# Pinning the accumulating transfers of the summed weights behind the GpSimd work named ahead of them

## The chip, the cores and the metric

The kernel runs on one core of one Trainium2 chip. The time is the device time of one execution in microseconds (us). It is measured in several runs, and the median counts. The core has five engines that run side by side, each working through its own queue in order: TensorE (PE, matrix products), VectorE (DVE), ScalarE (ACT), GpSimd (POOL) and SyncE (SP, which here only starts transfers). Transfers between main memory (HBM) and the on-chip memory (SBUF) are done by DMA engines; a queue starts them and goes on.

## The reference

A decoder trunk of two layers over 512 positions with 1024 channels in float32. Layer 0 mixes positions by causal mean pooling, layer 1 by attention in a sliding window of 128. Each mixer is followed by a gated MLP with a causal convolution of width 3:

```python
def conv_glu_ffn(h, w_in, conv_w, conv_b, w_out):
    u = h @ w_in                                  # 1024 -> 2 * 2816
    c = causal depthwise conv of u, width 3, + conv_b
    a, g = c[..., :D_FF], c[..., D_FF:]
    return (a * jax.nn.silu(g)) @ w_out           # 2816 -> 1024
```

Every mixer and every MLP reads `rms_norm(h, g) = h / sqrt(mean(h*h) + 1e-6) * g` and is added to `h`; a last norm closes the trunk.

## The kernel before

The activations lie with the 1024 channels on the partitions, as eight tiles `h0` to `h7` of 128x512. TensorE works on pairs: each float32 operand is split into a rounded part `h` and the rest `l`, and `mm3` (L83 to L87) makes one product of three matmuls: L85 is h times h, L86 and L87 are the cross terms. The split of a weight tile of 128x1024 is done in `weights` (L94): a transfer on SyncE's queue brings the raw tile (L91, a ring of three buffers), ScalarE copies it to the rounded part (L99), and VectorE subtracts to get the rest (L102). The split tiles have rings of four buffers each. For the first four weight tiles of layer 0 the subtraction is done on GpSimd instead, each in four pieces of 256 columns (`early_weights`, L319).

The norm before the MLP isn't applied ahead of the products. The activations are only scaled by the gain and split (`split_scaled`, L242 on ScalarE and L243 on VectorE, tiles `f0x_h` and `f0x_l`), and the factor 1/sqrt is multiplied in after the products. It comes from `Norm`: `add` squares each `h` tile on ScalarE (L212 for the first, L206 for the others, with two buffers `sq`) and adds it to one tile `n_acc` on GpSimd (L215, seven adds); `stats` sums over the channels by eight small matmuls on TensorE (L221) and takes the inverse root on VectorE (L181 to L195, `rs_` tiles); `spread` makes a diagonal of it (L231) and spreads it over the partitions by matmuls (L232) and a copy (L235).

`mlp_in` (L366) forms the 44 output tiles of `w_in`. In layer 0 it takes the first four weight tiles in two groups of two, and then one tile at a time. After the second group the statistics are issued (L395), after the fifth tile the spread (L397); only then can the products of these five tiles leave their banks (L358: times the factor, then the convolution, L361 to L363).

The product with `w_out` is done in three stretches (`GROUPS`), and two of them in each layer use sums of weight blocks and seven products of half size in place of eight (`mlp_sums`, L459). Their weights come from `sum_weights` (L438), four times for each stretch, sixteen times in all. It fills a tile `u` by a transfer on SyncE's queue (L447), and a second transfer, started by GpSimd, adds other blocks onto it while it is brought in (L450, `accum_op=ALU.add`). It therefore needs that L447 has landed. Tiles `r` and `q` come by L448 and L449. GpSimd then adds `u` and `r` into a tile `v` (L453, L454), and all four are split.

The order in each queue isn't the program's. A scheduler inside the compiler goes through the program with a model of how long instructions and transfers take, and gives each engine what is ready first in that model. On the chip each engine then works strictly in the order it was given, and waits where the model was wrong. `pin = tc.keep_in_program_order` (L116) binds one instruction behind the instruction that the program names last before it on the same engine. It orders the two in the queue and adds no wait. The instructions of the pooling mixer on ScalarE and VectorE are pinned in an order written out by hand (L341); the adds of the norm (L352) aren't, and neither are the transfers of L450.

Of the kernel before, what the change touches and what calls it, by code (L numbers as in the profile page):

```python
# [23 lines left out]
ALU = mybir.AluOpType  # L24
# [34 lines left out]
def trunk(ctx: ExitStack, tc: tile.TileContext, x_tok, x_t, vecs, w_pool, w_kq, w_v, w_o, w_in, w_out, w_sums, out_a, out_b):  # L59
    nc = tc.nc  # L60
    V, A, G, T = nc.vector, nc.scalar, nc.gpsimd, nc.tensor
# [32 lines left out]
    def weights(src, n, name, eng=None, raw=None, step=1024, pin=lambda ins: ins):  # L94

        raw = raw or fetch(src, n, name)
        h = wp.tile([P, 1024], F32R, tag="wh", name=f"{name}_h")
        l = wp.tile([P, 1024], F32R, tag="wl", name=f"{name}_l")
        pin(A.activation(h[:, :n], raw[:, :n], AF.Copy))  # L99
        for a in range(0, n, step):  # L100
            o = slice(a, min(a + step, n))
            (eng or V).tensor_tensor(l[:, o], raw[:, o], h[:, o].bitcast(F32), ALU.subtract)  # L102
        return h, l
# [7 lines left out]
    def out_weights(layer, m):  # L111
        n = 2 * GROUPS[layer][-1][0]
        w = weights(w_out[layer][m], n * P, f"wo{layer}_{m}")
        return [part(w, k) for k in range(n)]

    pin = tc.keep_in_program_order  # L116
# [38 lines left out]
    for g, w in enumerate(WINDOWS):  # L155
        b = band[:, g, :]
# [281 lines left out]
    def sum_weights(fp, layer, g, p, n):  # L438

        src = w_sums[layer][g][p]  # L440
        w = n * P
        name = f"ws{layer}_{g}_{p}"
        v = fp.tile([P, 1024], F32, tag="uv", name=f"{name}_u_raw", bufs=4)
        u, v = v, fp.tile([P, 1024], F32, tag="uv", name=f"{name}_v_raw", bufs=4)
        r = wp.tile([P, 1024], F32, tag="raw", name=f"{name}_r_raw", bufs=3)
        q = wp.tile([P, 1024], F32, tag="raw", name=f"{name}_q_raw", bufs=3)
        nc.sync.dma_start(u[:, : 2 * w].rearrange("p (a b) -> p a b", a=2), src[:, 0:4:2, :])  # L447
        nc.sync.dma_start(r[:, : 2 * w].rearrange("p (a b) -> p a b", a=2), src[:, 0:2, :])  # L448
        nc.sync.dma_start(q[:, :w], src[:, 3, :])  # L449
        G.dma_start(u[:, : 2 * w].rearrange("p (a b) -> p a b", a=2), src[:, 2:4, :], accum_op=ALU.add)  # L450
        R = weights(None, 2 * w, f"{name}_r", raw=r)
        Q = weights(None, w, f"{name}_q", raw=q)
        G.tensor_tensor(v[:, :w], u[:, w : 2 * w], r[:, :w], ALU.add)  # L453
        G.tensor_tensor(v[:, w : 2 * w], v[:, :w], r[:, w : 2 * w], ALU.add)  # L454
        W = weights(None, 2 * w, f"{name}_v", raw=v)
        U = weights(None, 2 * w, f"{name}_u", raw=u)
        return R, Q, W, U

    def mlp_sums(fp, layer, g, n, z):  # L459

        for p in range(NC // 2):
            R, Q, W, U = sum_weights(fp, layer, g, p, n)
            ba, be, bf = (bank("ps") for _ in range(3))
            lo, hi = slice(0, HS), slice(HS, S)
            sn = fp.tile([P, S], F32, tag="sn", name=f"sn{layer}_{g}_{p}")

            def product(out, w, b, t, start=True, stop=True):
                for i in range(n):
                    x = tuple(y[:, t, :] for y in z[i])
                    mm3(out, part(w, b * n + i), x, start and i == 0, stop and i == n - 1, skip_group_check=True)  # L470

            product(ba[:, lo], R, 0, 0)
            A.activation(sn[:, lo], ba[:, lo], AF.Copy)
            product(bf[:, lo], R, 1, 1)
            product(be[:, lo], Q, 0, 6)
            product(ba[:, lo], W, 0, 5, start=False)
            A.activation(sn[:, hi], ba[:, lo], AF.Copy)
            product(bf[:, hi], W, 1, 2)
            product(be[:, hi], U, 1, 3)
            product(ba[:, lo], U, 0, 4, start=False)  # L480
            h1, h2 = h[2 * p], h[2 * p + 1]
            V.tensor_tensor(h1, h1, sn, ALU.add)
            V.tensor_tensor(h1, bf, h1, ALU.add)
            V.tensor_tensor(h1[:, hi], h1[:, hi], be[:, hi], ALU.subtract)
            V.tensor_tensor(h2, be, h2, ALU.add)
            h22 = h2.rearrange("p (a b) -> p a b", a=2)
            V.tensor_tensor(h22, h22, ba[:, None, lo].to_broadcast([P, 2, HS]), ALU.subtract)
# [40 lines left out]
    with tc.tile_pool(name="ap", bufs=2) as ap:  # L528
# [53 lines left out]
        for c in range(2):  # L582
            u = ap.tile([P, S], F32, name=f"ku{c}", bufs=1)
# [170 lines left out]
        for i in range(NU + 4):  # L754
            base = AHEAD + i * RATE
            have = max(i - 4, 0)
            if i < NU:
                n, b = units[i]
# [21 lines left out]
    with tc.tile_pool(name="fp1", bufs=2) as fp:  # L780
# [31 lines left out]
        w = {m: out_weights(1, m) for m in range(NB, NC)}  # L812
# [116 lines left out]
```

## Time and profile before

| | |
|---|---|
| median of 3 runs | 920.04 us (919.86 to 920.27) |
| profiled execution | 919.19 us |
| its span | 917.4 us |
| mean granted clock of TensorE | 0.995 |
| TensorE busy | 904.5 us, 99% |
| VectorE busy | 681.7 us, 74% |
| ScalarE busy | 459.6 us, 50% |
| GpSimd busy | 192.7 us, 21% |
| transfers of L450 | 16, of which 12 of 512 KB; median 5.4 us from issue to landing |

The profile records one execution. All its times are in us from the start of the span, unless marked ns. A row of the timeline reads: start, length, engine, line of the kernel, operation, output<-inputs, form, and how many instructions were merged ("x8"); in brackets the idle time of the engine before it and what ended that. A row of the waits reads: who waited for whom, us in total, times, longest. In a row of the chain of waits the two numbers are start and length. A row of windows gives the window, its length, the busy time (and instructions) of PE, PEld (TensorE's weight loads), DVE, ACT and POOL, then the clock granted to TensorE as a share of full speed, and the share and rate of the DMA engines. The releaser in brackets is inferred: where several things were waited for, it is the last one by the profile.

### The profile page before, as it was taken

The numbers are of one execution on the slowest core, as the hardware profiler recorded it, in microseconds if no ns is written. First come the engines' busy times: TensorE is split into PE (matmuls) and PEld (weight loads), VectorE is DVE, ScalarE is ACT, GpSimd is POOL, SyncE is SP. The second block draws the span as 40 slices with busy tenths as digits, with TensorE's granted clock in tenths as the row PEclk, the third lists the DMA queues.
The fourth block names the chain that finished last, engine by engine and source line by source line (L and its number), as shares of the span: only waits on it lengthen the run. The fifth ranks groups of instructions, "written<-read, shape, count | busy, mean of one in ns | idle before, by whom it ended". The sixth has DMA issues, their size and how long they took to land.

```text
span 917.4 us, 13114 instructions
## 1 busy us (share of the span) xinstructions
PE 904.5 (99%) x4956; PEld 787.4 (86%) x4956; DVE 681.7 (74%) x1085; ACT 459.6 (50%) x715; POOL 192.7 (21%) x280
## 2 busy tenths in 40 slices
PE   9989999999999999999999999999999999999996
PEld 8878889988899888888889888888998889888896
DVE  7469998688997667555887472999977888877633
ACT  7646554344454344535888351654543445444532
POOL 3620113000321000425765041003210112000023
PEclk9989999999999999999999999999999999999999
DMA  8432436522444422322110043334464325523202
GB/s 328 124 114 69 134 100 170 172 93 92 115 127 125 131 78 80 127 93 92 47 47 24 12 151 85 100 115 138 126 165 134 96 72 117 175 93 98 93 18 92
DMA packets 33071, 100.03 MB, mean 109 GB/s; under 512 B 3440, under 2 KB 6000, under 8 KB 33008
## 3 DMA queue, kind: packets, MB, share of 16 engines
q1 hardware_dynamic: 30704, 91.33, 30.1%
q0 software_dynamic: 2304, 7.87, 5.2%
q8 instruction: 39, 0.64, 0.3%
q14 instruction: 24, 0.20, 0.1%
HBM read 97.09 MB, written 2.10 MB: 108 GB/s over the span
## 4 chain that ended last, share of the span: by engine, by line
PE 93%; ACT 3%; POOL 2%; DVE 1%; issue 1%; ACTq 0%; DVEq 0%
PE bank L85 29%; PE bank L87 29%; PE bank L86 29%; PE bank L700 1%; PE bank L728 1%; POOL n_acc L215 1%; PE bank L287 1%; PE bank L254 1%; POOL wi_l L102 1%; ACT h L331 0%; ACT sc L716 0%; ACT f0x_h L242 0%; ACT px_h L242 0%; ACT wi_h L99 0%; PE bank L221 0%
## 5 line engine op out<-in xcount | busy, mean ns | idle before, releaser
L99 ACT ACTIVATE wi_h<-wi_raw 128x1024 fp32r<-128x1024 f32 x88 | 93.0, 1060 | 133.6 <-PE bank L86 124.2
L102 DVE TENSOR_TENSOR wi_l<-wi_raw,wi_h 128x1024 fp32r<-128x1024 f32 x84 | 104.2, 1247 | 46.4 <-ACT wi_h L99 45.4
L87 PE MATMUL bank<-f0x_h,wi_l 128*128 128x512 f32 x352 | 137.8, 391 | 0.0
L86 PE MATMUL bank<-f0x_l,wi_h 128*128 128x512 f32 x352 | 137.7, 391 | 0.0
L85 PE MATMUL bank<-f0x_h,wi_h 128*128 128x512 f32 x352 | 137.4, 392 | 0.0
L85 PE MATMUL bank<-f1x_h,wi_h 128*128 128x512 f32 x352 | 137.2, 390 | 0.0
L86 PE MATMUL bank<-f1x_l,wi_h 128*128 128x512 f32 x352 | 137.0, 389 | 0.0
L87 PE MATMUL bank<-f1x_h,wi_l 128*128 128x512 f32 x352 | 137.0, 389 | 0.0
L358 DVE TENSOR_TENSOR c_u<-bank,n_rb 128x512 f32<-128x512 f32 x88 | 59.9, 686 | 45.0 <-PE bank L87 44.9
L453 POOL TENSOR_TENSOR ws_v_raw<-ws_u_raw,ws_r_raw 128x512 f32<-128x512 f32 (+1 forms) x16 | 22.9, 1432 | 324.2 <-DMA ws_r_raw<-w_sums 192.7
L215 POOL TENSOR_TENSOR n_acc<-n_acc,n_sq 128x512 f32<-128x512 f32 (+1 forms) x28 | 39.4, 1407 | 245.5 <-ACT n_sq L206 242.7
L87 PEld LDWEIGHTS bank<-f0x_h,wi_l 128*128 128x128 f32 x352 | 66.5, 189 | 14.3 <-POOL wi_l L102 0.4
L86 PEld LDWEIGHTS bank<-f0x_l,wi_h 128*128 128x128 f32 x352 | 66.7, 189 | 13.7
L85 PEld LDWEIGHTS bank<-f0x_h,wi_h 128*128 128x128 f32 x352 | 66.7, 189 | 13.7
L87 PEld LDWEIGHTS bank<-f1x_h,wi_l 128*128 128x128 f32 x352 | 66.1, 188 | 13.9
L86 PEld LDWEIGHTS bank<-f1x_l,wi_h 128*128 128x128 f32 x352 | 66.1, 188 | 13.6
L85 PEld LDWEIGHTS bank<-f1x_h,wi_h 128*128 128x128 f32 x352 | 66.1, 188 | 13.5
L361 ACT ACTIVATE c_t<-c_u,vec 128x512 f32<-128x512 f32 x88 | 70.1, 807 | 13.6 <-DVE c_u L358 12.7
L363 DVE SCALAR_TENSOR_TENSOR c_t<-c_u,vec,c_t 128x510 f32<-128x510 f32 x88 | 68.2, 779 | 2.3
L362 DVE SCALAR_TENSOR_TENSOR c_t<-c_u,vec,c_t 128x511 f32<-128x511 f32 x88 | 69.1, 789 | 0.5 <-ACT c_t L361 0.4
L428 ACT ACTIVATE zh<-y 128x256 fp32r<-128x256 f32 (+2 forms) x44 | 37.3, 847 | 60.6 <-DVE y L410 54.3
L401 ACT ACTIVATE c_t<-c_t 128x512 f32<-128x512 f32 x44 | 27.7, 629 | 58.8 <-DVE c_t L363 58.7
(210 smaller groups left out, 2185.2 us busy)
## 6 DMA issues: line engine op xcount, KB each, us to landing
wi_raw<-w_in SPq DMA_DIRECT2D x88, 512.0 KB, 3.5
ws_u_raw<-w_sums SPq DMA_DIRECT2D x12, 512.0 KB, 3.7
ws_u_raw<-w_sums POOLq DMA_DIRECT2D x12, 512.0 KB, 5.4
ws_r_raw<-w_sums SPq DMA_DIRECT2D x12, 512.0 KB, 3.5
kq_raw<-w_kq SPq DMA_DIRECT2D x10, 512.0 KB, 3.3
wo_raw<-w_o SPq DMA_DIRECT2D x8, 512.0 KB, 3.3
wo_raw<-w_out SPq DMA_DIRECT2D x8, 512.0 KB, 3.3
ws_q_raw<-w_sums SPq DMA_DIRECT2D x12, 256.0 KB, 2.7
```

The lines of the kernel that those rows point to most:

```text
L85: T.matmul(ps, lhsT=wh, rhs=xh, start=start, stop=False, **kw)
L86: T.matmul(ps, lhsT=wh, rhs=xl, start=False, stop=False, **kw)
L87: T.matmul(ps, lhsT=wl, rhs=xh, start=False, stop=stop, **kw)
L99: pin(A.activation(h[:, :n], raw[:, :n], AF.Copy))
L102: (eng or V).tensor_tensor(l[:, o], raw[:, o], h[:, o].bitcast(F32), ALU.subtract)
L215: eng.tensor_tensor(self.acc[:, lo:hi], self.acc[:, lo:hi], sq[:, lo:hi], ALU.add)
L358: V.tensor_tensor(u, ps, rb, ALU.mult)
L361: A.activation(t, u, AF.Identity, bias=col(V_CB + layer * 2 * NF + m), scale=cw[2])
L362: V.scalar_tensor_tensor(t[:, 1:], u[:, : S - 1], cw[1], t[:, 1:], ALU.mult, ALU.add)
L363: V.scalar_tensor_tensor(t[:, 2:], u[:, : S - 2], cw[0], t[:, 2:], ALU.mult, ALU.add)
L401: A.activation(conv[1], conv[1], AF.Silu)
L428: A.activation(h, src, AF.Copy)
```

## The change

One call in `sum_weights` is wrapped in `pin`:

```diff
         nc.sync.dma_start(u[:, : 2 * w].rearrange("p (a b) -> p a b", a=2), src[:, 0:4:2, :])
         nc.sync.dma_start(r[:, : 2 * w].rearrange("p (a b) -> p a b", a=2), src[:, 0:2, :])
         nc.sync.dma_start(q[:, :w], src[:, 3, :])
-        G.dma_start(u[:, : 2 * w].rearrange("p (a b) -> p a b", a=2), src[:, 2:4, :], accum_op=ALU.add)
+        pin(G.dma_start(u[:, : 2 * w].rearrange("p (a b) -> p a b", a=2), src[:, 2:4, :], accum_op=ALU.add))
```

Each of the sixteen accumulating transfers is bound behind the GpSimd instruction that the program names last before it. For the first in each layer that is the last add of the norm before the MLP (L215), for the others the second add of the sums before (L454). Nothing else in the program differs; the scheduler goes through the program again with these sixteen bonds.

## The prediction

> **What bounds the kernel now.** I read the page first, then the waits of TensorE, then the chain of waits around the longest of them, and last the timelines of single engines there.
>
> ```profile
> span 917.4 us, 13114 instructions
> ...
> PE 904.5 (99%) x4956; PEld 787.4 (86%) x4956; DVE 681.7 (74%) x1085; ACT 459.6 (50%) x715; POOL 192.7 (21%) x280
> ...
> PE 93%; ACT 3%; POOL 2%; DVE 1%; issue 1%; ACTq 0%; DVEq 0%
> ```
>
> TensorE is the bound: busy 99% of the span, and 93% of the chain. Something that moves on GpSimd can change the time only where TensorE stands still or runs slowly. The waits of TensorE, all that the view lists:
>
> ```profile
> PE bank L221 <- POOL n_acc L215: 3.2, 1, 3.2
> PE bank L254 <- DVE warm L252: 2.2, 1, 2.2
> PE bank L837 <- ACT n_sq L206: 0.5, 1, 0.5
> ```
>
> L254 is the start and L837 the tail. In between TensorE waits once, 3.2 us, and for GpSimd: L221 is the statistics of the first feed-forward norm, which need the sum of squares that GpSimd builds at L215. The granted clock in the windows around that wait:
>
> ```profile
> 48.00:49.00 1.00, 0.34 (x2) 0.00 (x0) 0.38 (x2) 1.00 (x2) 1.00 (x1) 1.00 0.00 0
> ...
> 50.00:51.00 1.00, 0.00 (x0) 0.00 (x0) 0.34 (x1) 0.00 (x0) 1.00 (x1) 0.84 0.67 270
> ...
> 57.00:58.00 1.00, 1.00 (x5) 0.82 (x4) 0.76 (x6) 0.00 (x0) 0.00 (x0) 0.75 1.02 311
> ```
>
> The number after the five engines is the clock: it falls within 50 to 51 and is back within 57 to 58. So the stall costs its own length and slow matmuls behind it. The chain there, and the same two steps in layer 1, where TensorE didn't wait:
>
> ```profile
> 47.12 2.15 POOL n_acc L215
> ...
> 49.34 2.13 POOL n_acc L215
> ...
> 51.51 1.87 PE bank L221 x8
> ...
> 60.94 0.89 PE bank L232 x8
> ```
>
> ```profile
> 571.19 0.79 PE bank L221 x8
> ...
> 577.58 0.89 PE bank L232 x8
> ```
>
> L221 to L232 is the statistics and 24 matmuls. It takes 9.43 us in layer 0 (60.94 - 51.51) and 6.39 in layer 1 (577.58 - 571.19). The lowered clock thus costs 3.04 us.
>
> **What moves.** GpSimd's timeline:
>
> ```profile
> 33.69 1.04 POOL L450 DMA_DIRECT2D ws_u_raw<-w_sums  x1 [5.93 <-DVE f0x_l L243]
> 34.48 5.83 POOL L102 TENSOR_TENSOR wi_l<-wi_raw,wi_h 128x256 fp32r<-128x256 f32 x8
> 40.05 11.41 POOL L215 TENSOR_TENSOR n_acc<-n_acc,n_sq 128x512 f32<-128x512 f32 x7
> 108.43 1.78 POOL L453 TENSOR_TENSOR ws_v_raw<-ws_u_raw,ws_r_raw 128x512 f32<-128x512 f32 x1 [56.97 <-DMA ws_r_raw<-w_sums]
> ...
> 111.85 0.89 POOL L450 DMA_DIRECT2D ws_u_raw<-w_sums  x1
> ...
> 551.85 1.50 POOL L215 TENSOR_TENSOR n_acc<-n_acc,n_sq 128x512 f32<-128x512 f32 x1 [3.94 <-ACT n_sq L206]
> 553.54 0.90 POOL L450 DMA_DIRECT2D ws_u_raw<-w_sums  x1 [0.20 <-issue]
> ```
>
> There are 16 transfers of L450. The pin sets each behind the GpSimd instruction that the program names last before it: L454 of the sums before, or the last L215 of the norm. The second (111.85), the first of layer 1 (553.54) and the others stand there already. Only the very first moves: from before the eight L102 pieces and seven L215 adds to behind them. Nothing needs it before L453 at 108.43, so its 1.04 us, its transfer and any wait of its own lie in 57 us of idle GpSimd: cost nothing. Without that cover it would cost its row, 1 us.
>
> What it held up is the point:
>
> ```profile
> 26.40 1.35 POOL L102 TENSOR_TENSOR wi_l<-wi_raw,wi_h 128x256 fp32r<-128x256 f32 x1
> 26.41 0.74 DVE L243 SCALAR_TENSOR_TENSOR f0x_l<-h,vec,f0x_h 128x512 fp32r<-128x512 f32 x1
> ...
> 28.21 0.65 SPq L447 DMA_DIRECT2D ws_u_raw<-w_sums  x1
> ...
> 28.45 1.07 ACT L99 ACTIVATE wi_h<-wi_raw 128x1024 fp32r<-128x1024 f32 x1
> 29.05 0.74 DVE L243 SCALAR_TENSOR_TENSOR f0x_l<-h,vec,f0x_h 128x512 fp32r<-128x512 f32 x1
> ...
> 30.01 1.07 ACT L99 ACTIVATE wi_h<-wi_raw 128x1024 fp32r<-128x1024 f32 x1
> 30.16 0.75 DVE L243 SCALAR_TENSOR_TENSOR f0x_l<-h,vec,f0x_h 128x512 fp32r<-128x512 f32 x1 [0.36 <-ACT f0x_h L242]
> ...
> 31.73 2.08 DVE L243 SCALAR_TENSOR_TENSOR f0x_l<-h,vec,f0x_h 128x512 fp32r<-128x512 f32 x3 [0.81 <-ACT f0x_h L242]
> ```
>
> ```profile
> DMA to landing us min/median/max: 4.7/5.2/5.6
> ```
>
> The transfer adds onto a tile that SyncE's L447 fills, issued at 28.21. The view of that tile shows two landings between 24 and 60 us; L447's took the 4.7, so it ends at 32.9, a little before L450 starts at 33.69. The profile blames DVE's f0x_l, which ended at about the same time; I take the landing. The eight pieces queued behind it have their inputs from 29.52 (28.45 + 1.07) and 31.08. Had they gone then, they would begin 4.96 us earlier than 34.48.
>
> Not all of that is kept. A piece alone takes 0.70 us (40.05 - 34.48, over 8), but the one at 26.40 took 1.35, ending 0.60 behind the L243 that started beside it (26.41 + 0.74). Four L243 start at 30.16 and later, and one ends at 29.79. Costs to GpSimd: 0.27 for that tail, and per L243 between 0 and 0.75. I take 0.6 each, the excess of the 1.35 row (0.65) rounded down because gaps lie between them: 2.4. Net gain of GpSimd 4.96 - 0.27 - 2.4 = 2.3 us; bounds 1.7 and 4.7.
>
> [...]
>
> The seven adds then follow as before, just earlier: their squares on ScalarE wait for GpSimd, and the two DVE splits that collide with the last two adds (2.15 and 2.13 us against 1.30 for an earlier one in the chain) hang on those squares too, so the pattern moves along.
>
> ```profile
> 45.75 1.30 POOL n_acc L215
> ```
>
> The chain of adds ends at 51.47 - 2.3 = 49.2 instead of 51.47 (49.34 + 2.13). TensorE arrives when its second group of weights is done:
>
> ```profile
> 33.22 0.39 PE L86 MATMUL bank<-f0x_l,wi_h 128*128 128x512 f32 x1
> ...
> 47.95 0.39 PE L87 MATMUL bank<-f0x_h,wi_l 128*128 128x512 f32 x1
> ```
>
> That is 48.34. New idle time: 0.85 us, between 0 and 1.5. The DVE rows that the earlier pieces may push back are read by TensorE only later: the f0x_l begun at 31.73 is needed at 33.22, 0.75 us after its end (31.73 + 0.74), and the next two later still, so a delay of 0.6 is covered; where it isn't, it falls inside this same idle time.
>
> **The clock.** If TensorE stands for 0.85 us instead of 3.17, I expect no fall: the fall in 50 to 51 came over 2 us after TensorE stopped at 48.34. [...] No run here shows a gap near 1 us.
>
> **The step after.** With the clock kept, L232 comes 6.39 us after the statistics. What is late next is the DVE work between them:
>
> ```profile
> 53.42 0.16 DVE L181 TENSOR_SCALAR rs_v<-bank 128x4 f32<-128x4 f32 x1 [3.08 <-PE bank L221]
> 53.53 1.23 DVE L102 TENSOR_TENSOR wi_l<-wi_raw,wi_h 128x1024 fp32r<-128x1024 f32 x1
> ...
> 54.74 1.22 DVE L102 TENSOR_TENSOR wi_l<-wi_raw,wi_h 128x1024 fp32r<-128x1024 f32 x1
> ...
> 57.91 0.88 DVE L231 TENSOR_SCALAR n_d<-ident,n_r 128x128 f32<-128x128 f32 x4
> 61.84 1.23 DVE L102 TENSOR_TENSOR wi_l<-wi_raw,wi_h 128x1024 fp32r<-128x1024 f32 x1 [3.05 <-ACT wi_h L99]
> ```
>
> From L181 to the first of L231's four pieces' end is 4.7 us (57.91 + 0.22 - 53.42), against 5.6 of matmuls (6.39 - 0.79): covered by 0.9. Behind L232 the same work follows relative to TensorE, which never waits again before the tail, so the gain is kept to the end.
>
> **Sum.** 3.17 - 0.85 = 2.3 of idle time and 3.04 of clock: 5.35 us, bounds 4.7 (idle 1.5) and 6.2 (idle 0). The profiled execution is 919.19 us (span 917.4 and 1.8 around it) and would come to 913.8; it lies 0.85 under the median of 920.04. From the median: 914.7, own range 913.8 to 915.4.
>
> **Rivals.**
>
> *The clock still falls.* A gap near 1 us, followed by eight tiny matmuls, may be enough. Then only idle time is saved: 2.3 us, 917.7. For it: the fall came at most 2.7 us after TensorE stopped (48.34 to 51), so less than 3 us of rest are enough. Against: layer 1 runs the same eight without a fall. Chance 0.14.
>
> *The transfer wasn't what held GpSimd.* The profile names f0x_l for the 5.93 us. If the pieces are shut out by DVE until the last L243 ends at 33.81, they begin only 0.67 us earlier; the gap stays 2.5 us, the clock falls, 919.4. Against: the piece at 26.40 passed in between L243s. The case that the pin changes no order at all ends here too, at 920.0. Chance 0.12.
>
> *Slower: the order on DVE turns over.* Each engine's order comes from a compile-time model, and the pin gives it other times. The DVE split of the ninth weight (61.84) stands behind L231. It needs TensorE's fifth group to end. If the model sets it ahead of the norm's steps, TensorE waits at L232 for a split that itself starts 0.9 us (61.84 - 60.94) after TensorE got there: L232 at about 49.2 + 6.39 = 55.6 would become 55.6 + 0.9 + 1.23 + 2.1 of norm steps (57.91 - 53.42 less the two splits between) + 0.2 = 60.0. That is 0.9 before today's 60.94, but TensorE has stood 4.4 us, and slow matmuls of 3.0 follow: 2.1 slower, 922.1. It decides if the split leaves its place behind L231. Against: today the split stands 3 us behind. Chance 0.09, with other turns of order that cost as much.
>
> **How the numbers follow.** Forecast 0.65. Within 0.2% (918.2 to 921.9, about what a measurement of this kernel can tell from no change) lie the second rival and the worst of the first. Faster 0.78, same 0.13, slower 0.09. The range reaches from 913.4, a little under idle 0 for the spread of runs, to 918.6, which takes in the first rival with the gap at its bound of 1.5.
>
> **What would show it.** Right: L450's first start behind the seventh L215, at 48 to 50; the first late L102 near 29.6, pieces of 1.0 to 1.35 beside L243; TensorE's wait at L221 under 1.5 us; the clock at 1.00 from 47 to 58; L221 to L232 near 6.4. Wrong: a start of those pieces after 33, a wait at L221 over 2 us, or a new wait at L232.

## The result and the profile after

The changed kernel takes 913.3 us (median of 4 runs, 913.19 to 914.04), the kernel before 920.15 us beside it (4 runs, 919.86 to 920.91). The ratio is 0.9926, with an interval of 0.9909 to 0.9943. The forecast was 914.7 us with a range from 913.4: the direction and the place were right, and the time fell 0.1 us below the range. The queues of the two programs differ in one place only: on GpSimd, the first L450 stands behind the seven adds.

The profiled execution after took 913.19 us. Its page, with the same lines as before:

```profile
span 911.4 us, 13112 instructions
...
PE 901.2 (99%) x4956; PEld 784.7 (86%) x4956; DVE 684.0 (75%) x1085; ACT 459.8 (50%) x715; POOL 192.8 (21%) x280
...
PE 92%; POOL 2%; DMA 2%; ACT 1%; issue 1%; DVE 1%; SPq 0%; ACTq 0%; POOLq 0%; DVEq 0%
```

The span is 6.0 us shorter, and TensorE's busy time fell by 3.3 us for the same 4956 matmuls: some of them ran faster. The waits of TensorE:

```profile
PE bank L254 <- DVE warm L252: 2.2, 1, 2.2
PE bank L837 <- ACT n_sq L206: 0.5, 1, 0.5
PE bank L287 <- DVE sband L285: 0.3, 1, 0.3
PE bank L221 <- POOL n_acc L215: 0.2, 1, 0.2
```

The wait at L221 is down from 3.2 to 0.2 us. GpSimd's timeline shows why:

```profile
29.58 7.48 POOL L102 TENSOR_TENSOR wi_l<-wi_raw,wi_h 128x256 fp32r<-128x256 f32 x8 [1.84 <-ACT wi_h L99]
37.03 11.24 POOL L215 TENSOR_TENSOR n_acc<-n_acc,n_sq 128x512 f32<-128x512 f32 x7
48.20 1.05 POOL L450 DMA_DIRECT2D ws_u_raw<-w_sums  x1
```

The eight pieces start at 29.58 instead of 34.48, as soon as ScalarE has the rounded part. They take 7.45 us to the first add instead of 5.57, with VectorE at its L243 meanwhile:

```profile
30.15 0.78 DVE L243 SCALAR_TENSOR_TENSOR f0x_l<-h,vec,f0x_h 128x512 fp32r<-128x512 f32 x1 [0.37 <-ACT f0x_h L242]
31.71 3.36 DVE L243 SCALAR_TENSOR_TENSOR f0x_l<-h,vec,f0x_h 128x512 fp32r<-128x512 f32 x3 [0.79 <-ACT f0x_h L242]
```

The last three L243 take 3.36 us instead of 2.08. Both engines lose: GpSimd 1.88 us, VectorE 1.28. The chain and the clock there:

```profile
46.12 2.16 POOL n_acc L215
...
48.32 1.05 PE bank L221 x8
...
54.96 0.89 PE bank L232 x8
```

```profile
50.00:51.00 1.00, 1.00 (x6) 0.81 (x5) 1.00 (x3) 0.00 (x0) 0.00 (x0) 1.00 0.98 143
...
57.00:58.00 1.00, 1.00 (x6) 0.81 (x6) 1.00 (x3) 0.28 (x1) 0.00 (x0) 1.00 0.00 0
```

The statistics begin 3.19 us earlier (51.51 - 48.32), L221 to L232 takes 6.64 us instead of 9.43, and the clock stays at 1.00. Together 5.98 us by L232, and it is kept to the end: the last ScalarE step of the chain starts at 912.75 before and 906.77 after, 5.98 apart.

```profile
906.77 0.69 ACT ob L853
```

### The profile page after: what moved, and what is told of

Its sections match the earlier page's. It is cut to its first block, busy times and chain, and to the rows that moved or that the text cites. A ratio compares the mean times of both kernels' runs of the same rounds, so it can differ in the third digit from the quotient of the medians.

```text
span 911.4 us, 13112 instructions
## 1 busy us (share of the span) xinstructions
PE 901.2 (99%) x4956; PEld 784.7 (86%) x4956; DVE 684.0 (75%) x1085; ACT 459.8 (50%) x715; POOL 192.8 (21%) x280
## 4 chain that ended last, share of the span: by engine, by line
PE 92%; POOL 2%; DMA 2%; ACT 1%; issue 1%; DVE 1%; SPq 0%; ACTq 0%; POOLq 0%; DVEq 0%
PE bank L85 30%; PE bank L86 29%; PE bank L87 29%; PE bank L700 1%; PE bank L728 1%; POOL wi_l L102 1%; DMA h<-x_t 1%; POOL n_acc L215 1%; DMA wi_raw<-w_in 1%; ACT sc L716 0%; PE bank L232 0%; PE bank L221 0%; ACT q L611 0%; ACT wo_h L99 0%; SPq L131 0%
## 5 line engine op out<-in xcount | busy, mean ns | idle before, releaser
L102 DVE TENSOR_TENSOR wi_l<-wi_raw,wi_h 128x1024 fp32r<-128x1024 f32 x84 | 104.3, 1247 | 40.1 <-ACT wi_h L99 39.8
L215 POOL TENSOR_TENSOR n_acc<-n_acc,n_sq 128x512 f32<-128x512 f32 (+1 forms) x28 | 39.5, 1410 | 245.1 <-ACT n_sq L206 242.2
L362 DVE SCALAR_TENSOR_TENSOR c_t<-c_u,vec,c_t 128x511 f32<-128x511 f32 x88 | 71.2, 814 | 0.5 <-ACT c_t L361 0.4
```

Of the source, the lines that this page charges most:

```text
L215: eng.tensor_tensor(self.acc[:, lo:hi], self.acc[:, lo:hi], sq[:, lo:hi], ALU.add)
L362: V.scalar_tensor_tensor(t[:, 1:], u[:, : S - 1], cw[1], t[:, 1:], ALU.mult, ALU.add)
```

## The experiments

**What GpSimd waited for.** My theory was that L450, waiting for the landing of L447, held the pieces. The rival was that VectorE's f0x_l, which the profile named, or the issue itself did. The first experiment keeps a transfer at the old place, but one that waits for nothing: a plain transfer into `v`. It leaves out the first accumulation; the other transfers are pinned.

```diff
+        if (layer, g, p) == (0, 0, 0):
+            with tc.issue_after(last_piece[0]):   # last piece of the second weight tile
+                G.dma_start(v[:, : 2 * w]..., src[:, 2:4, :])
+        else:
+            pin(G.dma_start(u[:, : 2 * w]..., src[:, 2:4, :], accum_op=ALU.add))
```

> The first transfer of L450 stays at its old place, between the pieces of the second and the third weight tile, but is a plain transfer into the tile v that waits for nothing; the first accumulation is left out, and the other transfers are pinned as in the change. Theory (the wait for the landing of L447 was the cost): GpSimd issues it at about 27.8, in the idle time ahead of the third tile, the pieces start at 29.6 as in the changed kernel, TensorE waits at L221 for 0.2 to 0.5 us, 913 to 914 us. Rival (a transfer at this place is held up by VectorE's L243, or its issue itself is what holds GpSimd): it starts near 33 or takes several us, the pieces start after it, 919 to 921 us.

Measured: 913.53 us (4 runs), a ratio to before of 0.9936 (0.9921 to 0.9951). GpSimd's timeline (the added lines move L450 to L461):

```profile
27.81 0.76 POOL L461 DMA_DIRECT2D ws_v_raw<-w_sums  x1
29.71 7.49 POOL L102 TENSOR_TENSOR wi_l<-wi_raw,wi_h 128x256 fp32r<-128x256 f32 x8 [1.14 <-ACT wi_h L99]
```

The transfer goes at once, in idle time, and the pieces follow with their inputs. An L243 of VectorE ran beside it from 27.84 on. The transfer stands at the same place of GpSimd's queue as in the kernel before, and its wait is gone. So neither the place nor the issue cost anything here; the wait did.

The second experiment moves the landing: one more transfer on SyncE's queue ahead of L447.

```diff
+        if (layer, g, p) == (0, 0, 0):
+            nc.sync.dma_start(v[:, : 2 * w]..., src[:, 0:4:2, :])
         nc.sync.dma_start(u[:, : 2 * w]..., src[:, 0:4:2, :])
...
+        ins = G.dma_start(u[:, : 2 * w]..., src[:, 2:4, :], accum_op=ALU.add)
+        if (layer, g, p) != (0, 0, 0):
+            pin(ins)
```

(In these two kernels the second L447 is pinned on SyncE's queue as well, to keep it from moving up.)

> The first transfer of L450 accumulates as before and isn't pinned (the others are), but SyncE starts one more transfer of 512 KB, into v, right ahead of L447, so that L447 lands some 1.5 to 2 us later. The scheduler puts L450 behind the third tile's four pieces, ahead of the fourth's. Theory (L450 waits for the landing): it starts at 34.5 to 35.5 instead of 33.69, the fourth tile's pieces follow it and end near 38.5 to 39.5, TensorE waits at L221 for 1.4 to 2.5 us, 914.5 to 918.5 us by whether the clock falls. Rival (L450 waits for VectorE's f0x_l): it starts at 33.7 as before, the wait at L221 is about 0.5 us, 913.5 us.

Measured: 918.46 us (10 runs, 916.37 to 919.71), ratio 0.9987 (0.9977 to 0.9997). GpSimd's timeline, where L450 is L454, and SyncE's transfer into `u` in the part on DMA issues (its last number is us to landing):

```profile
30.02 3.80 POOL L102 TENSOR_TENSOR wi_l<-wi_raw,wi_h 128x256 fp32r<-128x256 f32 x4 [1.84 <-ACT wi_h L99]
36.67 1.04 POOL L454 DMA_DIRECT2D ws_u_raw<-w_sums  x1 [2.85 <-PE bank L85]
37.46 3.09 POOL L102 TENSOR_TENSOR wi_l<-wi_raw,wi_h 128x256 fp32r<-128x256 f32 x4
```

```profile
29.34 0.59 SPq L449 DMA_DIRECT2D ws_u_raw<-w_sums  x1
```

```profile
ws_u_raw<-w_sums SPq DMA_DIRECT2D x1, 512.0 KB, 6.7
```

The start moved by 3 us, from 33.69 to 36.67, as the landing did (29.34 + 6.7 = 36.04, against 32.9); both moved further than I expected, and TensorE waits 3.2 us instead of the 1.4 to 2.5 forecast. It starts 0.6 us behind the landing, and 0.8 before. VectorE's last L243 had ended at 35.03, 1.6 us earlier. The name in brackets changed from f0x_l to a matmul, neither of which has to do with it. The theory holds. With four pieces ahead of the transfer instead of none, TensorE waits as long as before; but the transfer also started 3 us later, so what this order alone would give is not shown.

**What a shorter wait does to the clock.** The next kernels put known amounts of work on GpSimd into the changed kernel. First, the transfer behind the pieces and ahead of the adds (all sixteen are bound behind the last piece, in place of the pin; the queues differ from those of the changed kernel in the place of the first alone):

```diff
+        with tc.issue_after(last_piece[0]):   # last piece of the fourth weight tile
             G.dma_start(u[:, : 2 * w]..., src[:, 2:4, :], accum_op=ALU.add)
```

> The first transfer of L450 stands behind the eight pieces of L102 and ahead of the seven adds, with its wait long over; all else as in the changed kernel. Theory: only its issue of 1.05 us is paid, the adds end at 49.3 instead of 48.28, TensorE waits at L221 for 1.25 us. If the clock stands a wait of that length: 914.3 us, and L221 to L232 takes 6.4 to 6.7 us. Rival (the clock falls already then): L221 to L232 takes 9.4 us, 917.2 us.

Measured: 916.41 us (4 runs), ratio 0.9965 (0.9952 to 0.9979). The wait, the chain (L226 and L237 are L221 and L232) and the windows:

```profile
PE bank L226 <- POOL n_acc L220: 1.2, 1, 1.2
```

```profile
50.08 1.05 PE bank L226 x8
...
58.32 0.89 PE bank L237 x8
```

```profile
52.00:53.00 1.00, 1.00 (x4) 0.81 (x3) 1.00 (x3) 0.00 (x0) 0.00 (x0) 0.58 0.08 33
53.00:54.00 1.00, 1.00 (x4) 0.72 (x4) 0.98 (x4) 0.00 (x0) 0.00 (x0) 0.50 0.43 94
...
55.00:56.00 1.00, 1.00 (x5) 0.81 (x4) 0.82 (x5) 0.00 (x0) 0.00 (x0) 0.71 1.10 197
```

The wait is as expected, 1.2 us, but the clock falls after it: L226 to L237 takes 8.24 us, between my two numbers. The lowered stretch is 0.84 us in the window from 52 ((1 - 0.58) / 0.5), 2 us, and 0.58 us in that from 55: 3.4 us. By the same sum over the rows of before (0.32 us in the window from 50, half clock from 51 to 57, 0.5 in that from 57) it lasted 6.8 us there, twice as long. In issue_before_adds it began 2 us after TensorE had resumed.

Then memsets ahead of the last add, two and four of them:

```diff
         for c in range(NC):
+            for _ in range(2 if c == NC - 1 else 0):   # and 4
+                pin(G.memset(dly, 0.0))
             norm.add(c)                                # adds of n0 pinned
```

> The changed kernel with two memsets of 128x512 on GpSimd ahead of the last add (about 0.9 us), the adds pinned in their order. [...] Rival (a wait near 1 us is enough for the clock): L221 to L232 9.4 us, 917.2 us.

Measured: 913.57 us (4 runs), ratio 0.9938 (0.9921 to 0.9955), the wait at L221 0.3 us. The wait near 1 us that this was to test didn't come about, since the memsets cost nothing:

```profile
46.15 1.10 POOL L356 MEMSET dly<- 128x512 f32 x2
47.22 1.29 POOL L215 TENSOR_TENSOR n_acc<-n_acc,n_sq 128x512 f32<-128x512 f32 x1
```

The last add took 2.16 us in the changed kernel (46.12 to 48.28), beside VectorE's split (L102, 45.50 to 47.11). Here VectorE is busy from 46 to 47.29, the memsets run beside that split, and the add behind them takes 1.29. As a test of the clock this run says nothing beyond a wait of 0.3 us; it does show what a memset and an add cost beside VectorE.

> The same with four memsets (about 1.9 us): TensorE waits at L221 for about 2.1 us. [...] Rival (the clock falls at about 2 us): L221 to L232 9.4 us, 918.1 us; then the two together place the point between them.

Measured: 915.42 us (4 runs, 914.26 to 916.68), ratio 0.9958 (0.9943 to 0.9974). TensorE waits 1.4 us instead of the 2.1 expected, and the clock doesn't fall: L223 to L234 (L221 and L232 here) takes 6.64 us. That is a longer wait than in issue_before_adds, and no fall. So I profiled both kernels once more.

> The kernel with four memsets, profiled once more. In its first profile TensorE waited 1.4 us at L221 and the clock stayed; its times lie from 914.26 to 916.68 us. Theory: with a wait of this length it is a matter of where the windows of the clock lie, execution by execution, so the same kernel falls in some executions (L221 to L232 8.2 us, 916 us or more) and not in others (6.6 us, below 915). Rival: the clock never falls in this kernel and its times differ by the start alone; then 6.6 us always.

> The kernel with the transfer ahead of the adds, profiled once more. In its first profile TensorE waited 1.2 us and the clock fell for one window. Theory: 8.2 us again or 6.6 us, by where the windows lie. Rival (the clock falls in this kernel whenever TensorE waits 1.2 us): 8.2 us.

The chain in the first profile of delay_long, and in the second:

```profile
49.92 1.05 PE bank L223 x8
56.56 0.89 PE bank L234 x8
```

```profile
49.82 1.05 PE bank L223 x8
...
58.06 0.89 PE bank L234 x8
```

The same kernel, the same wait of 1.4 us: 6.64 us in one execution (914.71 us), 8.24 in the other (916.25). issue_before_adds gave 8.24 again (916.73 us), so the run doesn't tell whether it ever escapes. At this length the fall is a matter of the execution.

The traces also show what differs. In the profile of before the clock changes at 50.68, 57.51 and 914.25: 6.83 and 856.74 us apart, which is 2 and 251 times 3.413. I therefore count the executions in stretches of that length. In the second profile of delay_long one begins at the fall, at 51.26. The first profile has no fall here; its next change comes behind the last matmul, at 909.87, and 252 stretches before it one begins at 49.71. The stretches around the wait, two of the first profile and two of the second:

```profile
46.29:49.71 3.42, 2.20 (x10) 1.50 (x8) 1.21 (x1) 1.94 (x2) 3.25 (x6) 1.00 0.78 241
49.71:53.12 3.41, 3.20 (x18) 2.81 (x19) 2.11 (x4) 0.17 (x1) 1.13 (x2) 1.00 0.56 126
```

```profile
47.85:51.26 3.41, 1.99 (x13) 1.50 (x12) 0.35 (x2) 1.68 (x2) 2.83 (x4) 1.00 0.44 155
51.26:54.67 3.41, 3.41 (x9) 2.63 (x8) 3.24 (x11) 0.00 (x0) 0.00 (x0) 0.50 1.00 198
```

(The counts take in matmuls that began before the stretch, and the eight small ones.) In the first profile an edge fell into the wait: 8 matmuls of 512 columns start in the stretch before it and 10 in the one behind it, against 15 in a full one. In the second, the wait and the small matmuls lie in one stretch, and only 3 large ones start in it. Counted so around this wait, over all fourteen profiles, the clock is low behind each of the eleven stretches with 6 or fewer large matmuls, and full behind each with 7 or more. In the profile of before, 4 start in the stretch from 47.26 to 50.68 and 2 in the next, each followed by a low one, and 8 in the third, followed by the full clock. By this count, where the edges lie goes with whether the clock falls behind a wait of this length, and a second low stretch follows when the next one, too, holds only few. The count was made afterwards; no run was made to test it.

**Why the medians differ by more than the profiles.** The profiled executions differ by 6.0 us, the medians by 6.85.

> The changed kernel once more, in five rounds beside the kernel before. The two profiled executions differ by 5.98 us (919.19 to 913.19), the two medians by 6.85. Theory: the kernel before pays for its lowered clock by a different amount in each execution, and the profiled one paid little; then its times spread over about 1 us and go with the mean granted clock (a slower run has the lower clock), the changed kernel's times stay within 0.3 us, and the medians differ by 6 to 7 us. Rival: the 0.9 us are chance of the few runs; then no such relation, and the difference of the medians comes back to 6.0.

Measured: 913.69 us (5 runs, 913.63 to 913.91) against 919.5 (15 runs, 918.32 to 921.04), ratio 0.9936 (0.9924 to 0.9949). The kernel before spreads over 2.7 us, the changed one over 0.3 (0.85 in the four runs of the result), and the difference of the medians is 5.8. The times don't simply go with the mean granted clock: the four slowest runs of before (920.21 to 921.04 us) have 0.995, the six from 919.01 to 919.83 have 0.994. Three more profiles of the kernel before:

> The kernel before, profiled once more. Theory: the lowered clock behind the wait at L221 lasts one window of 3.4 us in some executions and two in others, by where the wait falls in windows that run on their own. With one window L221 to L232 takes about 8 us instead of 9.43 and the execution about 1.5 us less than one with two. Rival: it always takes 9.4 us, and the times differ by the start alone.

> The kernel before, a second time: as for the first, 8 or 9.4 us from L221 to L232 by the theory, 9.4 by the rival.

> The kernel before, a third time: as for the first, 8 or 9.4 us from L221 to L232 by the theory, 9.4 by the rival.

The chain in before_1 (918.46 us) and in before_2 (920.73 us):

```profile
51.93 1.05 PE bank L221 x8
60.15 0.89 PE bank L232 x8
```

```profile
52.66 1.87 PE bank L221 x8
62.40 0.89 PE bank L232 x8
```

TensorE waits 3.2 us in all. L221 to L232 takes 8.22 us in before_1, 8.25 in before_3 (918.69 us), 9.74 in before_2, and 9.43 in the profile that the prediction read: one lowered stretch or two. The start differs too: the first matmul of the feed-forward comes at 26.2 in three of the profiles and at 27.0 in before_2. Both parts of the expectations hold a share: the clock gives about 1.2 to 1.5 us of the spread, the start up to 0.8. Why the start differs is open.

**Is there more to gain?** What is left of the wait is 0.2 us. The splits of the third and fourth weight tile go to VectorE:

```diff
-            ws.append(in_weights(0, *pre[i], G, raws[i] if i < 3 else None, pin))
+            ws.append(in_weights(0, *pre[i], G if i < 2 else None, raws[i] if i < 3 else None, pin))
```

> The changed kernel with the splits of the third and the fourth weight tile (the eight pieces of L102) on VectorE instead of GpSimd. What is left of the wait at L221 after the change is 0.2 us. Theory: the seven adds start once the squares are there, near 34.5, end near 46, TensorE doesn't wait at L221 and nothing else gets shorter: 913.0 to 913.5 us, no difference that can be measured. Rival: VectorE's two splits of 1.2 us get between its L243 and TensorE starves in its first group: 914 us or more, with a wait before 48 us.

Measured: 915.32 us (4 runs), ratio 0.9953 (0.9937 to 0.997): slower than the change. TensorE doesn't wait at L221 any more, and waits at L232:

```profile
PE bank L232 <- DVE n_d L231: 1.0, 1, 1.0
```

```profile
50.81 0.16 DVE L183 TENSOR_SCALAR rs_i<-rs_v 128x4 int32<-128x4 int32 x1
52.66 1.23 DVE L102 TENSOR_TENSOR wi_l<-wi_raw,wi_h 128x1024 fp32r<-128x1024 f32 x1 [1.68 <-ACT wi_h L99]
```

```profile
51.56 1.06 ACT L99 ACTIVATE wi_h<-wi_raw 128x1024 fp32r<-128x1024 f32 x1 [2.61 <-DMA wi_raw<-w_in]
```

The split of a later weight stands between the norm's steps on VectorE, its copy on ScalarE waits for a transfer, and the norm waits behind it. Neither expectation named this wait. The scheduler had also set ScalarE's order anew, so it isn't shown that the moved splits alone did it. Nor does the wait explain all: it adds 0.8 us (1.0 against the 0.2 at L221), and the feed-forward also began 0.7 us later than in the changed kernel (26.84 against 26.18). The clock stays at 1.00 through this wait of 1.0 us; the two stretches that it touches hold 12 and 8 large matmuls.

## Why the prediction was nearly right, and where it failed

*What moves and what it held up:* right. Only the first L450 moved, its issue and transfer cost nothing behind the adds, and the wait for the landing was the cause (plain_no_wait, late_landing). The second rival, by which the profile's f0x_l held GpSimd, is refuted.

*The terms of the sum:* this is the step that failed. GpSimd's gain was mis-sized: 2.3 us forecast, 3.2 measured. I charged it 2.67 us for VectorE's L243 (0.27 and 4 x 0.6). It lost 1.88 (7.45 - 5.57), and VectorE paid as well: 1.28 us on its last three L243. I had reckoned as if GpSimd always gave way. In the profile after, both take longer where they meet:

```profile
32.19 1.18 POOL L102 TENSOR_TENSOR wi_l<-wi_raw,wi_h 128x256 fp32r<-128x256 f32 x1
32.70 1.23 DVE L243 SCALAR_TENSOR_TENSOR f0x_l<-h,vec,f0x_h 128x512 fp32r<-128x512 f32 x1
```

Undisturbed, the last pieces took 0.74 us each and an L243 0.75, so each L243 cost GpSimd about 0.44 us instead of 0.6. The adds ended 3.2 us earlier instead of 2.3, and TensorE waited 0.2 us instead of 0.85.

A small term I had put at nothing: in the kernel before, TensorE also came late to the statistics, because a piece of `wi_l` wasn't ready when it got there (0.35 us):

```profile
38.30 0.19 PEld L87 LDWEIGHTS bank<-f0x_h,wi_l 128*128 128x128 f32 x1 [0.35 <-POOL wi_l L102]
```

With the pieces earlier, it came there 0.24 us sooner (48.10 instead of 48.34). The clock's term was 2.79 instead of 3.04, since the statistics after the short wait took 1.05 us and not 0.79. The sum is 2.95 (the wait, 3.17 less 0.22) and 0.24 and 2.79, 5.98 instead of 5.35 us: 0.63 more, and within its bounds of 4.7 to 6.2.

*The range:* off the median of 920.04 the measured sum would still lie inside it (914.06); the base put the time outside. I took the sum off that median, though I had written that the profiled execution lay 0.85 us below it, and ended the range 0.4 us under the best sum. Part of what makes the kernel before vary is the very cost that the change removes: one or two lowered stretches of the clock. No profile of the changed kernel has one here. Off its own execution the sum gives 913.84, against 913.19 measured in the profiled execution after.

*The clock:* the forecast that it doesn't fall came true, but at a wait of 0.2 us, not at the 0.85 for which I made it; that is luck in part. My reason, that a wait of 0.85 would be safe, is not shown, and the runs speak for more than the 0.14 that I gave the first rival: at 1.2 and 1.4 us the clock fell in three of four profiles. A stretch that holds a wait of 0.85 and the eight small matmuls has room for (3.41 - 0.85 - 1.05) / 0.23, about 6.6, large ones: by the count above that is right at the edge (an estimate from these rows; 0.23 us is a large matmul's share of the chain at full clock). In issue_before_adds 1.2 us and the eight small matmuls were enough, in both of its profiles. In splits_on_vector a wait of 1.0 us, at L232, passed without a fall.

*The step after:* right for the change; L232 found its inputs. That its cover is thin shows in splits_on_vector, where it is the wait that comes next. The third rival's turn of order on VectorE didn't come: the order there is the same as before.

## What to carry to other kernels

The transfer that adds onto a tile waited here for the tile's first filling (it started 0.8 us behind the landing in before, 0.6 in late_landing), and it did so in the queue of the engine that issues it, with pieces behind it whose inputs were there from 29.52 on and which started at 34.48: put such a transfer behind the compute that is ready, not ahead of it. Price a stall of TensorE with the clock that it costs (here L221 to L232 took 6.64 us at the full clock and, in the kernel before, 8.22 to 9.74 with a fall), and expect that cost to differ from execution to execution; take a gain that removes it off the execution in which it was read. Where two engines slow each other down (here 1.88 us on GpSimd, 1.28 on VectorE), charge both.

## What the runs showed of the hardware

- Behind a wait of TensorE of 1.2 us (issue_before_adds, two profiles) and 1.4 us (delay_long, two profiles), followed by eight matmuls of two columns, the clock was at half for 3.4 us in three profiles of the four; behind a wait of 3.2 us in the kernel before it was so for 3.4 us (before_1, before_3) or 6.8 us (before, before_2).
- Around this wait the clock was low behind every stretch of 3.41 us in which 6 or fewer matmuls of 512 columns started (4 and 2 in before, 3 in delay_long_2), and full behind every one with 7 or more (8 in before, 8 and 10 in delay_long); counted over the fourteen profiles.
- Two GpSimd memsets took 1.10 us beside a VectorE split with two inputs in delay_short (four, half of them without one beside them, 2.27 in delay_long), while an add of GpSimd beside it took 2.16 us in the changed kernel, instead of 1.29 in delay_short.
- In the profile after, a GpSimd piece and a VectorE L243 that met took 1.18 instead of 0.74 us, and 1.23 instead of 0.75.
- The profile's name for the releaser of the waiting transfer was f0x_l in before and a matmul in late_landing; it started 0.8 and 0.6 us behind the landing that it waited for (33.69 against 32.9, 36.67 against 36.04).
